# Hybrid encoder trunk: layer 0's output weights serve two chunks at once

## The chip, the cores and the metric

The kernel runs on one core of a Trainium2 chip. Its engines are TensorE (PE in the profile, with PEld for its weight loads), VectorE (DVE), ScalarE (ACT), GpSimd (POOL) and SyncE (SP), which here only issues DMA transfers. The metric is the device time of one execution in microseconds (us), lower is better; medians of several runs are compared.

## The reference

Two layers of a bidirectional encoder on a sequence of 2048 tokens with 1024 channels, in float32, then a final RMSNorm:

```python
def hybrid_layer(x, ...):
    h = rmsnorm(x, norm_g)
    proj = einsum("bsd,de->bse", h, w_in)            # 1024 -> 3584
    ...
    y_a = conformer_conv(a_u, a_v, ...) * silu(a_z)  # depthwise conv of width 31, LayerNorm
    y_b = short_gated_conv(b_b, b_c, b_x, ...) * silu(b_z)
    y_c = window_gqa(c_q, c_k, c_v, sink) * silu(c_z)        # window of +-128 tokens
    y_d = neighborhood_attn(d_q, d_k, d_v, rpb) * silu(d_z)  # 32 x 64 grid
    y = concatenate([y_a, y_b, y_c, y_d], axis=-1)   # 4 x 256 channels
    return x + einsum("bse,ed->bsd", y, w_out)       # 1024 -> 1024
```

## The kernel before

Channels lie on partitions, tokens along the free dimension. The 2048 tokens are four chunks of 512; chunks 0 and 1 are half 0, chunks 2 and 3 half 1. Within a half the text calls the first chunk A and the second B. The core's memory holds the operand of two chunks at a time, in two slots: tiles s0h and s0l for A, s1h and s1l for B, eight tiles of 128 channels each (kept in four pairs).

Float32 products are made of three matmuls in the faster format: each operand is split into a high part (a cast on ACT) and a low part (a subtraction on DVE), and high x high, high x low and low x high are added up in PSUM. Weights come in tiles of 128 output channels; each is loaded in two halves of 256 KB into a raw tile (`load_w`, tile wraw, line 882) and split into whi and wlo (`split_w`).

The main work is a list of jobs. A job takes one weight tile and one chunk (24 matmuls of 128x512) or both chunks of the half (a joint job, 48 matmuls, the same weights split once). The order of the list is fixed: input jobs of half 0 and of half 1 of layer 0, output jobs of half 0 (layer 0), input jobs of half 0 of layer 1, output jobs of half 1 (layer 0), input jobs of half 1 of layer 1, output jobs of layer 1. `run(j)` emits a job in groups of 8 matmuls. After each group stands a point (`point()`), at which the generators of all the other work emit their next step: evictions (`evs`), attention units (`units`), and work in the background (`bg`), such as fetching the next input. Attention of a chunk is made of 16 units, each a chain of scores (s), softmax, transposes (pt) and values (o). If a job's operand has not been emitted when the job's turn comes, `idle_until` emits points without matmuls until it has. A scheduler then orders each engine's instructions by its own estimate of when they can start, so they don't stand exactly as emitted.

An output job of layer 0 adds its PSUM tile to a tile of x (`ev_out`: tile xo, fetched by `xo_tile`), squares the sum on ACT, adds the square to an accumulator (tile acc, tag "sa"), and stores the new x. After a chunk's eighth output job, `rstd_steps` sums the squares over the channels on PE (cs) and forms the reciprocal root in 13 small DVE steps; `stage_steps` of layer 1 reloads x (tile xt), spreads the root on PE (rb), copies it (rs) and scales the eight tiles; `place_steps` splits them into the slot. These are hung on the last output job of each chunk:

```python
then(o00[0], lambda: stage_steps(1, 0), pl(1, 0, 0))
then(o00[1], lambda: stage_steps(1, 1), pl(1, 1, 1))
```

In the same way y of chunk A is placed after A's last input job and y of B after B's (`place_y_steps`: loads of s0l or s1l from the tensors Y, a cast, a subtraction), once attention, convolution and gates of that chunk are done (`y_ready`). The input jobs begin with 3 (layer 0) or 5 (layer 1) tiles for A alone and then for B alone, go on with joint jobs, and end with 3 tiles for A and then B.

Of the kernel before, what the change touches and what calls it, by code (L numbers as in the profile page):

```python
# [7 lines left out]
F32 = mybir.dt.float32  # L8
# [7 lines left out]
DEPTH = 2  # L16
SEQ = 2048
DM = 1024
P = 128
KT = DM // P  # L20
CH = 512
# [34 lines left out]
TB, TH, XTB, GA, GB = 5, 2, 4, 2, 4  # L56
QSB, PRB, PTB = 2, 4, 2
GRP = 8
RU, RU1, RD = 3, 5, 3
PF, UNITS, SPACING = 7, 4, 5  # L60
PF_LATE, UNITS_LATE, SPACING_LATE = 3, 6, 2
LEAD, LEAD_LATE = 6.0, 6.0
# [9 lines left out]
def trunk(ctx, tc, xT, w_in, w_out, par, sink, rpb, fg, trig, cmask, dmask, out):  # L72
# [3 lines left out]
    def mkpool(name, bufs=1, **kw):  # L76
        return ctx.enter_context(tc.tile_pool(name=name, bufs=bufs, **kw))
# [3 lines left out]
    wp = mkpool("wp")  # L81
    gp = mkpool("gp")
# [6 lines left out]
    def T(pool_, shape, dt, tag, bufs, name=None):  # L89
        uid[0] += 1  # L90
        return pool_.tile(shape, dt, tag=tag, bufs=bufs, name=f"{name or tag}_{uid[0]}")
# [13 lines left out]
    def xrows(src, k, c):  # L105
        return src[2 * k * P:(2 * k + 2) * P, cs(c)].rearrange("(k p) t -> p k t", p=P)
# [63 lines left out]
    evs, bg, units, taps = [], [], [], deque()  # L170
# [33 lines left out]
    def idle_until(cond):  # L204
        n = 0
        while not cond():
            point()
            clk["pe"] += 1.8
            n += 1
            assert n < 4000, "nothing more happens"  # L210

    def hold(n):
        for _ in range(n):
            yield
# [610 lines left out]
    stat = {}  # L825

    def xo_tile(l, c, dt):
        src = xT if l == 0 else LP[l - 1]["X"]
        if l == DEPTH - 1:
            if c % 2 == 0:  # L830
                if dt % 2 == 0:
                    held["xx"] = T(gp, [P, 2, CH], F32, "xt", XTB, "xf")
                    sp.dma_start(out=held["xx"], in_=xrows(src, dt // 2, c))
                return held["xx"][:, dt % 2]
            if dt >= 4:
                if dt % 2 == 0:
                    held["xg"] = T(gp, [P, GW], F32, "gA", GA, "xf")
                x = held["xg"][:, (dt % 2) * CH:(dt % 2) * CH + CH]
            else:
                x = T(gp, [P, CH + 3], F32, "gB", GB, "xf")[:, :CH]  # L840
        else:
            x = T(gp, [P, CH + 3], F32, "gB", GB, "xo")[:, :CH]
        sp.dma_start(out=x, in_=src[dt * P:(dt + 1) * P, cs(c)])
        return x

    xos = {}

    def ev_out(l, dt, c, pt):
        x = xos[(l, c, dt)]
        dve.tensor_tensor(out=x, in0=x, in1=pt, op=ALU.add)  # L850
        yield
        if dt == 0:
            acc = stat[(l, c)] = T(gp, [P, CH], F32, "sa", 1, "acc")
            act.activation(out=acc, in_=x, func=AF.Square)
        else:
            acc = stat[(l, c)]
            sq = T(gp, [P, CH], F32, "t", TB, "sq")
            act.activation(out=sq, in_=x, func=AF.Square)
            if dt < KT - 1:
                dve.tensor_tensor(out=acc, in0=acc, in1=sq, op=ALU.add)  # L860
        yield
        if l < DEPTH - 1:
            sp.dma_start(out=LP[l]["X"][dt * P:(dt + 1) * P, cs(c)], in_=x)
        if dt == KT - 1:
            yield from rstd_steps(l + 1, c, (acc, sq), ("rc", l + 1, c))
            if l == DEPTH - 1:
                yield
                rb = spread(RC[l + 1][:, 4 * c:4 * c + 4], CH)
                yield
                rs = rb  # L870
                for k in range(KT):
                    xk = xos[(l, c, k)]
                    dve.scalar_tensor_tensor(out=xk, in0=xk, scalar=fg_t[:, k:k + 1], in1=rs, op0=ALU.mult, op1=ALU.mult)
                    sp.dma_start(out=out[k * P:(k + 1) * P, cs(c)], in_=xk)
                    if k % 2:
                        yield


    def load_w(jb, hf):
        raw = T(wp, [P, 4, P], F32, "wraw", 4)  # L880
        jb.setdefault("raw", []).append(raw)
        sp.dma_start(out=raw, in_=jb["src"][:, 4 * hf:4 * hf + 4, :])

# [5 lines left out]
    jobs = []  # L889

    def job(src, keys, ev, pre=None, post=None):
        jobs.append({"src": src, "keys": keys, "ev": ev, "pre": pre, "post": post})
# [98 lines left out]
        return first, len(jobs) - 1  # L991

    def out_jobs(l, half):
        ends = []
        for c in ((0, 1), (2, 3))[half]:
            for dt in range(KT):
                def pre(dt=dt, c=c):
                    if l == DEPTH - 1 and c % 2:
                        idle_until(lambda: not taps)

                    def get():
                        yield from hold(2)
                        for d in ((0, 1, 2) if dt == 0 else (dt + 2,)):
                            if d < KT:
                                xos[(l, c, d)] = xo_tile(l, c, d)
                    bg.append(get())
                job(w_out[l, dt], [("y", l, c)], lambda c_, pt, dt=dt: ev_out(l, dt, c_, pt), pre, None)
            ends.append(len(jobs) - 1)
        return ends

    def y_ready(l, c):
        need = [(k, l, c, p, j) for k in "dc" for p in range(2) for j in range(4)]
# [197 lines left out]
```

## Time and profile before

| | us |
|---|---|
| Median of 3 runs | 2041.24 (2040.83 to 2048.28) |
| The profiled execution | 2040.77 |
| its span, first to last instruction | 2039.0 |
| PE busy in the span | 1959.9 |
| DVE busy | 1489.6 |
| ACT busy | 1043.3 |
| POOL busy | 150.5 |

PE is busy for 96% of the span and its mean granted clock is 0.986 of full speed. Matmuls overlap their successors, so a busy share counts a wait only from where the last matmul ends. 1.8 us of the execution lie outside the span.

### The profile page before, as it was taken

Reading aid. Unit: us, or ns where it says so; the run is one execution under the profiler, and the core shown is the slowest. Engines: PE = TensorE matmul, PEld = TensorE weight load, DVE = VectorE, ACT = ScalarE, POOL = GpSimd, SP = SyncE. Lnnn points to the kernel's source line nnn. Section 1 sums busy time; section 2 is a strip of 40 time slices with the busy share of each in tenths; the row PEclk is TensorE's granted clock in tenths of the full one; section 3 lists DMA queues with packets and bytes.
Section 4 is the critical chain, followed back from the end, with each engine's and each line's share of the span. In section 5 each row is a group of like instructions: output and inputs, shape, how many; then the busy total and the mean of one; then the engine's idle time right before and its main releaser. Section 6 shows DMA issues by size and latency. Waiting matters only on the chain.

```text
span 2039.0 us, 29509 instructions
## 1 busy us (share of the span) xinstructions
PE 1959.9 (96%) x9600; PEld 1642.2 (81%) x9600; DVE 1489.6 (73%) x3209; ACT 1043.3 (51%) x2219; POOL 150.5 (7%) x138
## 2 busy tenths in 40 slices
PE   6999999999999999999999999999999889989997
PEld 5778888778788888878888888888888778878886
DVE  7444699947985777776465999777986457877775
ACT  5335434423365456556564445644237455777632
POOL 0241000043010100000010000001001000100000
PEclk9999999999999999999999999999999999999998
DMA  6995532588356369877663446876446874678473
GB/s 208 294 332 184 148 111 84 171 265 263 129 176 195 123 193 298 268 229 232 208 201 121 141 142 203 266 237 222 136 147 210 236 203 130 195 226 238 150 266 119
DMA packets 235003, 402.76 MB, mean 198 GB/s; under 512 B 26977, under 2 KB 92129, under 8 KB 234593
## 3 DMA queue, kind: packets, MB, share of 16 engines
q1 hardware_dynamic: 234848, 400.87, 63.1%
q8 instruction: 77, 1.26, 0.3%
q14 instruction: 78, 0.63, 0.1%
HBM read 299.78 MB, written 105.61 MB: 199 GB/s over the span
## 4 chain that ended last, share of the span: by engine, by line
PE 75%; DMA 13%; DVE 6%; issue 2%; ACT 2%; SPq 1%; POOL 1%; DVEq 0%; ACTq 0%; POOLq 0%
PE mm L135 61%; PE o L135 4%; PE s L135 4%; PE pt L734 3%; DMA prob<-bias 2%; DMA wraw<-in_w_out_dram 2%; DMA s1l<-Y 2%; DVE wlo L128 1%; DVE accA L128 1%; PE cs L135 1%; POOL bmo L817 1%; PE rb L135 1%; DMA vt<-VD 1%; DMA Y<-accA 1%; DMA s0l<-Y 1%
## 5 line engine op out<-in xcount | busy, mean ns | idle before, releaser
L135 PE MATMUL mm<-s1h,whi 128*128 128x512 f32 x1152 | 458.3, 398 | 16.5 <-ACT whi L218 8.3
L135 PE MATMUL mm<-s1h,wlo 128*128 128x512 f32 x1152 | 456.8, 397 | 2.0 <-DVE wlo L128 1.9
L135 PE MATMUL mm<-s0h,whi 128*128 128x512 f32 x1152 | 453.9, 394 | 4.9 <-ACT whi L218 3.0
L135 PE MATMUL mm<-s1l,whi 128*128 128x512 f32 x1152 | 456.0, 396 | 0.0
L135 PE MATMUL mm<-s0l,whi 128*128 128x512 f32 x1152 | 454.3, 394 | 1.8 <-DVE s0l L128 1.8
L135 PE MATMUL mm<-s0h,wlo 128*128 128x512 f32 x1152 | 454.1, 395 | 0.4 <-DVE wlo L128 0.4
L218 ACT CAST whi<-wraw 128x512 fp32r<-128x512 f32 x408 | 251.8, 618 | 393.0 <-PE mm L135 294.6
L128 DVE TENSOR_TENSOR wlo<-wraw,whi 128x512 fp32r<-128x512 f32 x408 | 293.5, 721 | 161.3 <-ACT whi L218 149.1
L128 DVE SCALAR_TENSOR_TENSOR accA<-gA,par,accA 128x1024 f32<-128x1024 f32 (+1 forms) x240 | 309.0, 1305 | 0.7
L135 PEld LDWEIGHTS mm<-s1h,whi 128*128 128x128 f32 x1152 | 219.6, 191 | 62.2 <-ACT whi L218 9.5
L135 PEld LDWEIGHTS mm<-s1h,wlo 128*128 128x128 f32 x1152 | 219.6, 191 | 47.9 <-DVE wlo L128 3.8
L135 PEld LDWEIGHTS mm<-s1l,whi 128*128 128x128 f32 x1152 | 220.1, 191 | 44.5 <-issue 0.5
L135 PEld LDWEIGHTS mm<-s0h,whi 128*128 128x128 f32 x1152 | 217.4, 189 | 47.7 <-ACT whi L218 4.1
L135 PEld LDWEIGHTS mm<-s0l,whi 128*128 128x128 f32 x1152 | 217.4, 189 | 45.6 <-DVE s0l L128 2.5
L135 PEld LDWEIGHTS mm<-s0h,wlo 128*128 128x128 f32 x1152 | 217.5, 189 | 44.4 <-DVE wlo L128 2.1
L707 ACT ACTIVATE prob<-prob,mn 128x384 f32<-128x384 f32 (+4 forms) x256 | 155.5, 608 | 113.2 <-DVE mn L128 111.2
L724 ACT ACTIVATE prob<-prob,sm 128x384 f32<-128x384 f32 (+4 forms) x256 | 142.2, 603 | 39.7 <-DVE sm L128 33.9
L128 DVE TENSOR_TENSOR pth<-pt,pth 128x512 fp32r<-128x512 f32 (+3 forms) x248 | 138.0, 572 | 29.0 <-ACT pth L218 28.0
L218 ACT CAST pth<-pt 128x512 fp32r<-128x512 f32 (+3 forms) x248 | 115.1, 496 | 80.3 <-PE pt L734 46.5
L135 PE MATMUL s<-ks,qs 128*128 128x384 f32 (+4 forms) x512 | 128.3, 352 | 17.6 <-DVE mn L128 10.9
L135 PE MATMUL o<-pth,vt 128*128 128x256 f32 (+2 forms) x784 | 129.8, 292 | 2.2 <-DVE oy L128 0.5
L135 PEld LDWEIGHTS o<-pth,vt 128*128 128x128 f32 (+2 forms) x784 | 114.9, 193 | 13.3 <-ACT prob L707 1.6
(122 smaller groups left out, 2006.0 us busy)
## 6 DMA issues: line engine op xcount, KB each, us to landing
wraw<-in_w_in_dram SPq DMA_DIRECT2D x280, 256.0 KB
wraw<-in_w_out_dram SPq DMA_DIRECT2D x128, 256.0 KB
qs<-QD SPq DMA_DIRECT2D x128, 128.0 KB
qs<-QC SPq DMA_DIRECT2D x128, 128.0 KB
G<-g SPq DMA_DIRECT2D x48, 256.0 KB
vt<-VD SPq DMA_DIRECT2D x144, 72.0 KB
xt<-in_xT_dram SPq DMA_DIRECT2D x20, 512.0 KB
KD<-t SPq DMA_DIRECT2D x32, 256.0 KB
```

The lines of the kernel that those rows point to most:

```text
L128: return fn(*a, **kw)
L135: pe.matmul(out=out, lhsT=lhsT, rhs=rhs, start=start, stop=stop)
L218: act.copy(out=hi, in_=src)
L707: act.activation(out=t[:, hh, :n], in_=t[:, hh, :n], func=AF.Exp, bias=mn[:, hh:hh + 1], scale=-1.0, accum_out=sm[:, hh:hh + 1])
L724: act.activation(out=t[:, hh, :n], in_=t[:, hh, :n], func=AF.Copy, scale=sm[:, hh:hh + 1])
L734: pe.transpose(out=tp[:kw, b_, hh, :], in_=t[:, hh, kb * kw:(kb + 1) * kw], identity=ident)
L817: pool.tensor_tensor(out=t[:, hh, :sz].rearrange("p (g r c) -> p g r c", r=rr, c=C), in0=mkv, in1=Ms[2 * p + hh][:, r0:r0 + R, c0:c0 + C]. ...
```

## The change

The output jobs of a half of layer 0 were eight for A and then eight for B, each splitting its own weights. Now the first two tiles (RO = 2) are done for A and then for B, the next four as joint jobs, and the last two for A and then for B: 12 jobs in place of 16. Layer 1 keeps its order. Since both chunks' sums of squares are open at once, there are two accumulators; the memory for the second comes from the raw weight tiles, now three. The tile of x is fetched when its own job begins, not from two jobs ahead on.

```diff
-RU, RU1, RD = 3, 5, 3
+RU, RU1, RD, RO = 3, 5, 3, 2
...
-            acc = stat[(l, c)] = T(gp, [P, CH], F32, "sa", 1, "acc")
+            acc = stat[(l, c)] = T(gp, [P, CH], F32, "sa", 2, "acc")
...
-        raw = T(wp, [P, 4, P], F32, "wraw", 4)
+        raw = T(wp, [P, 4, P], F32, "wraw", 3)
...
     def out_jobs(l, half):
-        ends = []
-        for c in ((0, 1), (2, 3))[half]:
-            for dt in range(KT):
-                def pre(dt=dt, c=c):
-                    if l == DEPTH - 1 and c % 2:
-                        idle_until(lambda: not taps)
-
-                    def get():
-                        yield from hold(2)
-                        for d in ((0, 1, 2) if dt == 0 else (dt + 2,)):
-                            if d < KT:
-                                xos[(l, c, d)] = xo_tile(l, c, d)
-                    bg.append(get())
-                job(w_out[l, dt], [("y", l, c)], lambda c_, pt, dt=dt: ev_out(l, dt, c_, pt), pre, None)
-            ends.append(len(jobs) - 1)
-        return ends
+        A, B = ((0, 1), (2, 3))[half]
+        ends = {}
+
+        def emit(dt, cc):
+            def pre():
+                if l == DEPTH - 1 and dt >= 2:
+                    idle_until(lambda: not taps)
+                for c in cc:
+                    if (l, c, dt) not in xos:
+                        xos[(l, c, dt)] = xo_tile(l, c, dt)
+            job(w_out[l, dt], [("y", l, c) for c in cc], lambda c_, pt: ev_out(l, dt, c_, pt), pre, None)
+            for c in cc:
+                ends[c] = len(jobs) - 1
+
+        if l == DEPTH - 1:
+            for c in (A, B):
+                for dt in range(KT):
+                    emit(dt, (c,))
+            return ends[A], ends[B]
+        for c in (A, B):
+            for dt in range(RO):
+                emit(dt, (c,))
+        for dt in range(RO, KT - RO):
+            emit(dt, (A, B))
+        for c in (A, B):
+            for dt in range(KT - RO, KT):
+                emit(dt, (c,))
+        return ends[A], ends[B]
```

How this moves instructions is seen in the built programs, at three places. The first is on PE, in the output jobs of half 0. Before, the third job (mm_1456) goes on with chunk 0:

```order
L135 MATMUL o_1437_7270<-pth_1426_7222,vt_1247_6454 128x256 x2
L734 MATMUL pt_1446_7316<-ident_77,prob_1403_7115 120x128 x4
L734 MATMUL pt_1447_7321<-ident_77,prob_1403_7115 120x128 x2
L135 MATMUL mm_1456_7340<-s0h_1370_6997,whi_1442_7287 128x512
L135 MATMUL mm_1456_7340<-s0l_1374_7001,whi_1442_7287 128x512
```

Now the third and fourth jobs (mm_1493 and mm_1510) are chunk 1's. These rows stand where they begin on the second half of their channels, tiles s1h_1466 and s1l_1470, the third pair of chunk 1's y; mm_1528, of which a row stands ahead, is the fifth job's part for chunk 0:

```order
L135 MATMUL mm_1528_7636<-s0h_1371_6998,wlo_1512_7577 128x512
L135 MATMUL o_1482_7436<-pth_1478_7411,vt_1458_7353 128x256 x2
L734 MATMUL pt_1487_7468<-ident_77,prob_1459_7358 128x128 x4
L135 MATMUL o_1482_7436<-pth_1479_7414,vt_1458_7353 128x256 x2
L135 MATMUL mm_1493_7486<-s1h_1466_7382,whi_1451_7330 128x512
L135 MATMUL mm_1510_7562<-s1h_1466_7382,whi_1506_7554 128x512
L135 MATMUL mm_1493_7486<-s1l_1470_7386,whi_1451_7330 128x512
```

Chunk 1's y is read from the third job on, where before it was read from the ninth; the first halves of the third to fifth jobs and attention stand ahead of the second halves. From the first output matmul to the first row with s1h_1466 there are 84 matmuls of jobs and 70 of attention (8 s of 360 columns, 8 s of 512, 26 o, 28 pt).

The second place is on PE, from the output jobs of half 1 to the input jobs of layer 1. Before, the last output job (mm_2864) is followed by the first input job (mm_2872) directly:

```order
L135 MATMUL mm_2864_13744<-s1h_2639_12716,whi_2861_13738 128x512
L135 MATMUL mm_2864_13744<-s1l_2643_12720,whi_2861_13738 128x512
L135 MATMUL mm_2864_13744<-s1h_2639_12716,wlo_2862_13739 128x512
L135 MATMUL mm_2872_13790<-s0h_2819_13532,whi_2865_13756 128x512
L135 MATMUL mm_2872_13790<-s0l_2823_13536,whi_2865_13756 128x512
```

Now two jobs of chunk 3 stand between chunk 2's last output job and the first input job for chunk 2 (mm_2834), with chunk 2's cs between the two jobs, and its rb and chunk 3's cs behind them. These rows are the end of that cs and what follows:

```order
L135 MATMUL cs_2817_13668<-ones_78,acc_2698_13013 128x1
L135 MATMUL cs_2817_13668<-ones_78,sq_2815_13663 128x1
L135 MATMUL mm_2834_13745<-s0h_2824_13708,whi_2807_13625 128x512
L135 MATMUL mm_2849_13800<-s0h_2824_13708,whi_2835_13756 128x512
L135 MATMUL mm_2834_13745<-s0l_2828_13712,whi_2807_13625 128x512
```

Eight jobs stood between the two before; the first two input jobs (mm_2834 and mm_2849) now take the tiles in turn. From half 0 into layer 1 it is the same, with 33 matmuls of attention between (8 s, 12 pt, 13 o) beside two jobs, two cs and rb.

The third place is on SP, near the start. Before:

```order
L882 DMA wraw_45_297<-in_w_in_dram 128x512
L882 DMA wraw_50_317<-in_w_in_dram 128x512
L273 DMA xt_83_490<-in_xT_dram 128x2x512
L273 DMA xt_84_492<-in_xT_dram 128x2x512
L273 DMA xt_85_494<-in_xT_dram 128x2x512
L273 DMA xt_86_496<-in_xT_dram 128x2x512
L882 DMA wraw_58_362<-in_w_in_dram 128x512
```

And now:

```order
L882 DMA wraw_45_297<-in_w_in_dram 128x512
L273 DMA xt_83_490<-in_xT_dram 128x2x512
L273 DMA xt_84_492<-in_xT_dram 128x2x512
L273 DMA xt_85_494<-in_xT_dram 128x2x512
L273 DMA xt_86_496<-in_xT_dram 128x2x512
L882 DMA wraw_50_317<-in_w_in_dram 128x512
L882 DMA wraw_58_362<-in_w_in_dram 128x512
```

With one raw tile less, the load of wraw_50 stands behind four loads of x.

## Rows read from the trace of the kernel before

**Rows 1.** The page, part 1: busy time, share of the span and instructions of each engine.

```profile
PE 1959.9 (96%) x9600; PEld 1642.2 (81%) x9600; DVE 1489.6 (73%) x3209; ACT 1043.3 (51%) x2219; POOL 150.5 (7%) x138
```

**Rows 2.** Busy time by stretch: stretch, length, engines' us, granted clock, DMA share, GB/s.

```profile
765.00:888.00 123.00, 117.24 (x582) 97.41 (x581) 87.87 (x206) 73.97 (x154) 1.29 (x1) 0.99 0.90 280
1262.00:1380.00 118.00, 116.28 (x589) 97.62 (x587) 91.17 (x229) 66.10 (x136) 2.89 (x2) 1.00 0.80 247
880.00:890.00 10.00, 7.30 (x30) 5.80 (x31) 7.49 (x22) 7.12 (x17) 0.00 (x0) 0.83 0.80 277
```

**Rows 3.** PE's waits from 765 to 888 us: us in total, times, longest.

```profile
PE mm L135 <- ACT whi L218: 2.9, 2, 2.1
PE mm L135 <- DVE wlo L128: 1.9, 1, 1.9
```

**Rows 4.** The page, part 5: groups of instructions; after the bar busy us, mean ns.

```profile
L218 ACT CAST whi<-wraw 128x512 fp32r<-128x512 f32 x408 | 251.8, 618 | 393.0 <-PE mm L135 294.6
L128 DVE TENSOR_TENSOR wlo<-wraw,whi 128x512 fp32r<-128x512 f32 x408 | 293.5, 721 | 161.3 <-ACT whi L218 149.1
```

**Rows 5.** Timeline of PE, output jobs of half 0: start us, us, instruction.

```profile
765.51 0.47 PE L135 MATMUL mm<-s0h,whi 128*128 128x512 f32 x1
765.82 0.39 PE L135 MATMUL mm<-s0l,whi 128*128 128x512 f32 x1
766.05 0.39 PE L135 MATMUL mm<-s0h,wlo 128*128 128x512 f32 x1
...
779.29 0.64 PE L135 MATMUL s<-ks,qs 128*128 128x512 f32 x2
...
781.52 0.48 PE L135 MATMUL mm<-s0h,whi 128*128 128x512 f32 x1
```

**Rows 6.** Timelines of ACT, SP and DVE: chunk 1's y is cast, stored, split.

```profile
772.09 1.14 ACT L218 CAST s1h<-s1l 128x512 fp32r<-128x512 f32 x2 [0.23 <-DMA s1l<-Y]
...
788.37 0.42 SPq L782 DMA_DIRECT2D Y<-ag  x1
...
798.85 0.69 DVE L128 TENSOR_TENSOR s1l<-s1l,s1h 128x512 fp32r<-128x512 f32 x1 [4.83 <-ACT s1h L218]
```

**Rows 7.** Timelines of DVE, then SP: chunk 2 from its last eviction on.

```profile
1325.40 0.69 DVE L128 TENSOR_TENSOR xo<-xo,mm 128x512 f32<-128x512 f32 x1 [1.60 <-PE mm L135]
...
1333.27 0.16 DVE L128 TENSOR_SCALAR rn<-cs 128x4 f32<-128x4 f32 x1 [0.39 <-PE cs L135]
...
1335.64 0.17 DVE L128 TENSOR_SCALAR rc<-rc 128x4 f32<-128x4 f32 x1
...
1342.38 5.39 DVE L128 SCALAR_TENSOR_TENSOR xt<-xt,par,rs 128x512 f32<-128x512 f32 x8 [1.47 <-ACT rs L302]
...
1348.29 0.68 DVE L128 TENSOR_TENSOR s0l<-xt,s0h 128x512 fp32r<-128x512 f32 x1
...
1331.40 0.38 SPq L863 DMA_DIRECT2D X<-xo  x1
...
1335.84 0.38 SPq L273 DMA_DIRECT2D xt<-X  x1
```

**Rows 8.** Timeline of PE, chunk 0: sums over channels, and the root spread.

```profile
835.38 0.28 PE L135 MATMUL cs<-ones,acc 128*128 128x1 f32 x2
...
836.86 0.36 PE L135 MATMUL cs<-ones,sq 128*128 128x1 f32 x2
...
848.62 1.05 PE L135 MATMUL rb<-ident,rc 128*128 128x128 f32 x8
```

**Rows 9.** The page, part 5: two groups of attention.

```profile
L724 ACT ACTIVATE prob<-prob,sm 128x384 f32<-128x384 f32 (+4 forms) x256 | 142.2, 603 | 39.7 <-DVE sm L128 33.9
L128 DVE TENSOR_TENSOR pth<-pt,pth 128x512 fp32r<-128x512 f32 (+3 forms) x248 | 138.0, 572 | 29.0 <-ACT pth L218 28.0
```

**Rows 10.** Waits of SP's queue and of PE over the whole span.

```profile
SPq L882 <- DVE wlo L128: 384.3, 177, 10.9
PE mm L135 <- ACT whi L218: 11.3, 6, 3.1
```

## Prediction, on record before the changed kernel ran

> **What bounds the kernel now.** I read the page first: TensorE (PE) is busy for 1959.9 of 2039.0 us [rows 1], so time is to be had only where PE stands still, and time is lost wherever a change makes it stand still. Then I read the two stretches that the change rewrites: the output projection of half 0 of layer 0 (765 to 888 us, "out phase 0") and that of half 1 (1262 to 1380 us, "out phase 1"). PE is busy for 117.2 of 123 us in the one and for 116.3 of 118 us in the other, with the DMA engines at 0.90 and 0.80 [rows 2]. So 5.8 and 1.7 us are idle there. In phase 0 the list of PE's waits puts 2.9 us on the high halves of the weights (whi) and 1.9 us on the low halves (wlo) [rows 3]: late weights. Last I read the timelines at the edges of these phases, because the change moves when chunk B's y is first wanted, and when chunk A's x is done.
>
> **Prices.** A 128x512 matmul starts 0.23 us after the one before it (765.82 to 766.05), so a single job (24 of them) is 5.5 us; one attention unit's four s, six o and six pt matmuls take 779.29 to 781.52, 2.2 us, or 0.14 us each [rows 5]. The sums over columns (cs) take 835.38 to 837.22, 1.85 us, and the spread of the result (rb) 1.05 us [rows 8].
>
> **What is removed.** Eight jobs fewer are split, four in each half: 16 halves of weights, each a 256 KB load, a cast of 618 ns on ScalarE (ACT) and a subtraction of 721 ns on VectorE (DVE) [rows 4]: 9.9 us of ACT, 11.5 us of DVE, 4 MB. All of it lies beside PE and is worth only the waits it causes. The matmuls stay the same in number. I take it that the weight waits of phase 0 (2.9 + 1.9 us) go, with the drop of the clock behind them: from 880 to 890 us the granted clock averages 0.83 [rows 2], so 1.7 us are lost beside the wait. And the 1.7 us of phase 1 go. Together -8.2 us; bounds 0 and -11 (all idle time of both phases, 7.5, the clock, and 1.7 more just behind phase 0).
>
> By the Trainium skill, Perfetto Trace Analysis, section Identifying the Most-Contended Engine, the busy share of matmuls says little about what is left, and that of weight loads should be used. Weight loads are busy for 97.4 of 123 us in phase 0, which would leave 25.6 us to gain and give about 2015 us. The start-to-start times above contradict it here: a load is hidden under each 0.23 us matmul, and nothing is gained by shortening loads. The sum goes by the rows.
>
> **What is moved, place A: the third job of an out phase.** Before, chunk B's y was wanted after eight jobs; now after two. In phase 0 the first job starts at 765.5 us [rows 5]. By the changed order, 84 main matmuls (the two jobs, and the first halves of the third, fourth and fifth, which the scheduler has put ahead) and 70 of attention stand before the first that reads the third pair of B's tiles: 84 x 0.23 + 70 x 0.14 = 29.1 us, so PE is there at 794.6 us. The first two pairs are cast from 772.09 us on at the latest; the third waits for the store of group C's rows (788.37) and is split at 798.85 [rows 6]. PE waits 4.2 us. Lower bound 0, if attention's last unit of chunk 1 ends earlier with fewer matmuls around it; upper bound 10, if the three units now packed into these 29 us wait for DVE and ACT in turn. In phase 1 the changed order puts B's first matmuls between those of the second job, so that B's y hardly comes too late there: 0.5 us (0 to 3).
>
> **Place C: from phase 1 into layer 1.** Before, eight jobs of B (55 us) covered the making of A's next input; now two do. The chain in the trace: A's last eviction at 1325.40, squares, cs, thirteen small DVE steps from 1333.27 to 1335.81 (2.5 us), rb, a copy (rs), eight scalings (5.4 us from 1342.38), first split at 1348.29 to 1348.97 [rows 7]: 23.6 us in all, with waits for PE in it. In the new order, from A's last matmul: B's first job 5.5, cs 1.85, B's second job 5.5 (the 2.5 us of small steps lie under it), rb 1.05, copy 0.7, scalings 5.4, split 0.7: 20.7 us. PE has 5.5 + 1.85 + 5.5 + 1.05 + 1.85 (B's sums) + 0.5 = 16.2 us of work. It waits 4.5 us; bounds 3 and 10 (23.6 less two jobs and the sums). The last X store and the reload behind it took 4.4 us (1331.40 to 1335.84) plus the landing, and fit under B's two jobs. Behind the first split PE has six matmuls per tile (1.4 us; the order takes two jobs in turn) against 0.68 us for a split, so nothing more is lost.
>
> **Place B: from phase 0 into layer 1.** The same chain, with attention in the queues: on PE 0.7 us more in B's first job, 1.4 us in the second and 0.7 us behind it; on ACT two row scalings (603 ns) stand ahead of the copy; on DVE a softmax step and two subtractions (572 ns) stand between the scalings and the first split [rows 9]: 20.7 + 0.7 + 1.4 + 0.7 + 1.2 + 0.6 + 1.1 = 26.4 us. PE's share in it is 48 main matmuls, two cs, rb and 33 of attention: 11.0 + 3.7 + 1.05 + 4.6 + 0.5 = 20.8 us. It waits 5.6 us; bounds 0 and 12.
>
> **The clock.** The waits at A, B and C are each about as long as the two waits of phase 0 on weights together [rows 3], whose drop of the clock cost 1.7 us: 3 x 1.7 = 5.1 us (0 to 6.8).
>
> **Three raw weight tiles.** Every raw load may go out only when the half three (not four) before it is split, half a single job (2.7 us) later, in all 408 halves, and SP has whatever follows queued behind that wait: it waited for wlo 177 times, 384.3 us in all, with four tiles already [rows 10]. The work that hides it is the job in between. Where PE waits on weights already, a later load adds its 2.7 us: six times on whi, 11.3 us in all [rows 10]. Six times 2.7 is 16 us, the upper bound; lower bound 0. I take 2.5, about one of the six, since SP's waits show that even now loads go out as a tile comes free, and PE was late only these six times.
>
> **At nothing:** the second accumulator of squares (both chunks' are alive at once); the tile of x, now fetched by its own job and not two ahead (a store and reload of 256 KB took 4.4 us, under a job's 5.5; if later, DVE waits in the eviction and the weights' subtractions behind it wait too); PSUM, of which a joint job takes two of three buffers, as it did before in the input phases.
>
> **Sum.** 4.2 + 0.5 + 4.5 + 5.6 + 5.1 - 8.2 + 2.5 = +14.2 us. The profiled execution took 2040.8 us, 0.5 us below the median of the three runs (2041.2), so **2055 us**; this case's own range is 2044 to 2066.
>
> **The rivals.**
> - *The covers are thin* (0.12): the three places cost their upper bounds, 10 + 3 + 10 + 12 and 6.8 for the clock, +42; nothing of phase 0's waits is won: about 2084. For it speaks that the old chain took 23.6 us with no one in a hurry; against it, the order, which shows PE's other work standing ahead.
> - *The third raw tile was needed* (0.13): the six waits on weights each grow by 2.7 us, 16 in place of 2.5: 2069. The Trainium skill, DMA: Bandwidth & Descriptors, section Rules for kernel authors, bears on it: issue a DMA early and wait for it late. Against it: PE waited for whi only six times in 408 halves.
> - *It cancels* (0.22): with attention ahead and DVE lighter, A costs 0, B 2, C 4.5, one drop of the clock 1.7, and -8.2 is won: 2041.
> - *Faster* (0.08): A, B and C stay below 1 us in all, because B's y and A's x are ready when wanted, and the waits of both phases go (-10.9): 2030. It needs PE's work ahead of place C to be 4.5 us longer than the rows give, so I hold it unlikely. Of the chance, 0.02 stands for the 2015 us that the Trainium skill's measure would give.
> - The forecast has the rest, 0.45.
>
> About 0.5% (10 us) is what a measurement can tell from no change. Slower by more: the two slow rivals and three quarters of the forecast's range, 0.59; within: 0.33; faster: 0.08. The range leaves out about one in ten at each end: 2035 to 2080.
>
> **What would show it.** In the changed profile: 392 halves of weights cast (408 less 16); PE's waits on s1h or s1l at the third out job of half 0, and on s0h or s0l at the first two input jobs of layer 1 in both halves, 4 to 6 us each, with the clock low behind each; no whi or wlo wait at the end of phase 0. It is wrong if those waits are missing, or if PE waits on whi elsewhere by more than 16 us in all.

## The result, and the profile after

The changed kernel takes 2072.01 us (median of four, 2068.66 to 2075.44) against 2041.03 for the kernel before (four runs, 2038.89 to 2048.28): ratio 1.0145, 95% interval 1.0119 to 1.017. That is 31 us slower, where +14 was forecast. The page's busy times (columns as in [rows 1]) of the execution that was profiled, the slowest of the four, with a span of 2073.6 us:

```profile
PE 1972.1 (95%) x9600; PEld 1653.1 (80%) x9600; DVE 1476.7 (71%) x3193; ACT 1035.9 (50%) x2203; POOL 149.8 (7%) x138
```

PE runs the same 9600 matmuls as in [rows 1]. Its idle time in the span rose from 2039.0 - 1959.9 = 79.1 to 2073.6 - 1972.1 = 101.5 us (+22.4), and it is busy 12.2 us longer on the same work: that is the clock, whose mean fell from 0.986 to 0.978. DVE and ACT have less to do, as forecast (12.9 and 7.4 us), and the kernel is slower all the same. Busy times by stretch (out phase 0, layer 1 half 0, out phase 1, the rest), first of the kernel before, cut at the phases' ends, then of the changed one:

```profile
765.50:887.40 121.90, 116.14 (x575) 96.43 (x574) 86.94 (x202) 72.87 (x152) 1.29 (x1) 0.99 0.90 279
887.40:1262.70 375.30, 373.82 (x1894) 317.17 (x1892) 282.63 (x627) 209.66 (x479) 12.65 (x9) 1.00 0.58 179
1262.70:1379.50 116.80, 115.08 (x583) 96.88 (x583) 89.97 (x228) 64.97 (x134) 2.51 (x2) 1.00 0.80 250
1379.50:2039.00 659.50, 625.59 (x3109) 523.63 (x3107) 479.99 (x1098) 352.19 (x764) 26.01 (x20) 0.98 0.62 190
```

```profile
767.30:903.60 136.30, 127.77 (x651) 108.29 (x650) 87.18 (x224) 78.26 (x171) 1.30 (x1) 0.96 0.81 247
903.60:1293.80 390.20, 381.08 (x1879) 321.03 (x1878) 289.04 (x647) 214.20 (x489) 13.11 (x9) 0.98 0.57 174
1293.80:1411.00 117.20, 112.39 (x537) 93.54 (x537) 72.36 (x164) 48.96 (x90) 6.75 (x5) 0.97 0.67 217
1411.00:2073.60 662.60, 623.68 (x3092) 524.11 (x3092) 481.02 (x1104) 351.13 (x763) 19.29 (x16) 0.97 0.62 188
```

Out phase 0 grew by 14.4 us, but layer 1 half 0, in which no code was changed, by 14.9. Out phase 1 grew by 0.4 and the rest by 3.1; 1.8 us were lost before 767. Each kernel was traced once, and this first stretch took 760.7 to 770.2 us in the traces cut in this way, so that a few us in one stretch say little without the waits behind them. Over the three phases PE's idle time went from 9.0 to 22.5 us and its busy time from 605.0 to 621.2, with 15 matmuls more on record (3067 for 3052; attention runs earlier): 13.5 us of waits, and some 14 of clock (16.2, less 15 x 0.14 for these). What PE waited for in the first two stretches, in the third, and from 1411 to 1425 us:

```profile
PE mm L135 <- ACT s1h L218: 5.1, 1, 5.1
PE mm L135 <- DVE wlo L128: 2.5, 1, 2.5
PE cs L135 <- ACT sq L858: 0.6, 1, 0.6
...
PE o L135 <- DVE pth L128: 3.1, 2, 2.9
PE mm L135 <- ACT t L372: 2.2, 1, 2.2
PE s L135 <- DVE wlo L128: 1.8, 1, 1.8
...
PE mm L135 <- ACT whi L218: 4.4, 3, 3.9
...
PE mm L135 <- DVE s0l L128: 3.9, 1, 3.9
```

The first row is place A (796 us), the first of the second stretch place B (904 us, 2.9 of it), the last place C: the waits that were forecast. At place B what PE met first was not s0h or s0l but attention's pth (the split transposes), which DVE splits at 906.61 us, behind the scalings of chunk A's x. Three were not: wlo at 880 us, the waits on t and behind wlo between 959 and 970 us, and whi at 1310 us.

The new code also changes a thing in layer 1, whose order it keeps. There the wait for the last convolution steps (`taps`) stood ahead of every output job of B; now it stands ahead of every output job from the third tile on, of A and of B. The traces show no cost of it: layer 1's output jobs take 250.4 us in both kernels (1788.6 to 2039.0 and 1823.2 to 2073.6 us).

**The weights at 880 us.** In [rows 3] PE waits for whi and wlo, and the prediction took both for late weights. The two long ones stand in one place, and they have two causes. PE, then ACT, before:

```profile
880.84 0.50 PE L135 MATMUL mm<-s1h,whi 128*128 128x512 f32 x1 [2.07 <-ACT whi L218]
883.43 0.71 PE L135 MATMUL mm<-s1h,wlo 128*128 128x512 f32 x1 [1.86 <-DVE wlo L128]
880.17 0.62 ACT L218 CAST whi<-wraw 128x512 fp32r<-128x512 f32 x1 [4.11 <-DMA wraw<-in_w_out_dram]
```

The whi was late because its load was: the cast on ACT waited 4.11 us for it. The load went out on SP at 874.27 us, behind a fetch of xo at which SP had stood for 5.8 us, until a store of X was done (from 866 to 880 us):

```profile
SPq L843 <- DMA X<-xo: 5.8, 1, 5.8
```

In the changed kernel that wait on whi is gone. The wait on wlo is another matter, and DVE's timeline tells why. Before:

```profile
875.33 0.14 DVE L128 TENSOR_TENSOR es<-mn,sink 128x2 f32<-128x2 f32 x1
882.08 0.28 DVE L128 TENSOR_TENSOR oy<-o,ou 64x128 f32<-64x128 f32 x1 [6.61 <-issue]
882.10 0.06 DVE L128 MEMSET cx<- 128x2 f32 x1
882.37 0.28 DVE L128 TENSOR_TENSOR oy<-o,ou 64x128 f32<-64x128 f32 x1
882.69 0.69 DVE L128 TENSOR_TENSOR wlo<-wraw,whi 128x512 fp32r<-128x512 f32 x1
```

After:

```profile
871.96 0.28 DVE L128 SCALAR_TENSOR_TENSOR ag<-oy,ag 128x128 f32<-128x128 f32 x1
881.95 0.06 DVE L128 MEMSET cx<- 128x2 f32 x1 [9.70 <-DMA X<-xo]
882.02 0.69 DVE L128 TENSOR_TENSOR wlo<-wraw,whi 128x512 fp32r<-128x512 f32 x1
```

A memset of two columns (60 ns) for cx, the padded operand of a convolution some 300 us later, has been put into DVE's queue here. In the built program it stands ahead of oy and wlo in the kernel before too, though oy's record begins 20 ns earlier. Its buffer belongs to the ring (gB) that the tiles xo use, and comes free only when a store of X is done. All of DVE waits, with it the split of the next weights into wlo, and PE behind them. The Trainium skill, PSUM — Partial Sum Buffer, section Engine vs sequencer instructions, says that VectorE's queue is strictly first in, first out; the 9.7 us for a 60 ns instruction agree.

**The stop at 956 to 970 us.** PE's timeline between the second and the third input job of chunk B in layer 1 (the 87th of the list, as the expectations count):

```profile
955.61 0.39 PE L135 MATMUL mm<-s1h,wlo 128*128 128x512 f32 x1
955.83 0.52 PE L135 MATMUL s<-ks,qs 128*128 128x384 f32 x2
...
958.14 0.38 PE L414 MATMUL tv<-ident,vt 128*128 128x128 f32 x2
...
961.14 1.04 PE L135 MATMUL s<-ks,qs 128*128 128x288 f32 x4 [1.84 <-DVE wlo L128]
963.04 0.69 PE L734 MATMUL pt<-ident,prob 128*128 128x128 f32 x2 [0.87 <-DVE hv L128]
...
964.12 1.11 PE L414 MATMUL tv<-ident,vt 128*128 128x128 f32 x4
...
966.10 1.48 PE L734 MATMUL pt<-ident,prob 128*96 128x128 f32 x6
969.77 0.79 PE L135 MATMUL mm<-s1h,whi 128*128 128x512 f32 x1 [2.19 <-ACT t L372]
```

For 14 us no job runs, only attention and the transposes of v (tv). These belong to chunk A's third input job: ACT copied its result (vt) at 929.6 us, and its tv runs at 958.1. In the kernel before the two were 912.7 and 918.5. Before, then after (windows 905 to 985 and 920 to 1000 us):

```profile
L414 PE MATMUL tv<-ident,vt x16: 270/272/273, 918.5 to 965.6; 128*128 128x128 f32 x16
...
L414 PE MATMUL tv<-ident,vt x16: 270/272/473, 958.1 to 993.5; 128*128 128x128 f32 x16
```

The tiles tv take turns with attention's own transposes in a ring of two PSUM buffers ("pt"), and here two late attention units stand ahead. Behind tv the chain goes on: its result (hv) is split and stored, its buffer lets ACT empty the PSUM tile of A's fifth job (t, which waited 1.08 us for that store), and that PSUM tile is what B's third job needs. The clock fell with it:

```profile
962.10:975.80 13.70, 10.49 (x33) 8.31 (x33) 7.40 (x20) 8.80 (x21) 0.00 (x0) 0.50 0.91 272
```

0.50 of full speed, 1.2 GHz, for 13.7 us, of which PE was busy 10.5.

**The wait at 1310 us** is made on ACT: the cast of whi (1313.24) stands behind casts of chunk 3's y, which wait 2.57 us for their load, and then waits 0.90 us for its own.

```profile
1311.21 1.14 ACT L218 CAST s1h<-s1l 128x512 fp32r<-128x512 f32 x2 [2.57 <-DMA s1l<-Y]
1313.24 0.62 ACT L218 CAST whi<-wraw 128x512 fp32r<-128x512 f32 x1 [0.90 <-DMA wraw<-in_w_out_dram]
```

### The profile page after: what moved, and what is told of

It is laid out like the page before. It is cut to its first block, busy times and chain, and to the rows that moved or that the text cites. A ratio compares the mean times of both kernels' runs of the same rounds, so it can differ in the third digit from the quotient of the medians.

```text
span 2073.6 us, 29400 instructions
## 1 busy us (share of the span) xinstructions
PE 1972.1 (95%) x9600; PEld 1653.1 (80%) x9600; DVE 1476.7 (71%) x3193; ACT 1035.9 (50%) x2203; POOL 149.8 (7%) x138
## 4 chain that ended last, share of the span: by engine, by line
PE 78%; DMA 12%; DVE 5%; issue 2%; ACT 1%; POOL 1%; SPq 1%; DVEq 0%; POOLq 0%; ACTq 0%
PE mm L135 64%; PE o L135 4%; PE s L135 4%; PE pt L734 3%; DMA prob<-bias 2%; DMA wraw<-in_w_in_dram 1%; DMA rep<-in_rpb_dram 1%; DMA VD<-hv 1%; DVE accA L128 1%; POOL bmo L817 1%; DMA bm<-rep 1%; DVE xt L128 1%; DVE wlo L128 1%; DMA s0l<-Y 1%; PE rb L135 1%
## 5 line engine op out<-in xcount | busy, mean ns | idle before, releaser
L218 ACT CAST whi<-wraw 128x512 fp32r<-128x512 f32 x392 | 242.0, 618 | 414.2 <-PE mm L135 296.9
L128 DVE TENSOR_TENSOR wlo<-wraw,whi 128x512 fp32r<-128x512 f32 x392 | 280.2, 716 | 187.3 <-ACT whi L218 174.5
L135 PE MATMUL o<-pth,vt 128*128 128x256 f32 (+2 forms) x784 | 131.7, 294 | 4.8 <-DVE pth L128 3.4
```

Source lines behind the costliest of these rows:

```text
L128: return fn(*a, **kw)
L135: pe.matmul(out=out, lhsT=lhsT, rhs=rhs, start=start, stop=stop)
L218: act.copy(out=hi, in_=src)
```

## The experiments

The theories, as the expectations number them. 1: the edges (places A, B, C) cost the time, and what follows them. 2: the third raw weight tile. 3: the planner (the code of `run`, `point` and `idle_until`, which lays the program out before it runs) starts attention units at the points at which it waits for staged operands, and the chip can't keep up. 4: the zero fill of cx. 5: the PSUM ring that v's transposes share with attention. Ratios are to the kernel before, run beside each.

### Two terms by themselves

**e1.**

```diff
-        raw = T(wp, [P, 4, P], F32, "wraw", 4)
+        raw = T(wp, [P, 4, P], F32, "wraw", 3)
```

> The kernel before with three raw weight tiles in place of four, and nothing else changed. If the edges of the out phases cost the time (theory 1), this is worth what the changed kernel had lost when it reached its first out phase, 1.5 us at 766 us, and about as much again behind it: 2041 to 2046 us. If the third raw tile was needed (theory 2), the six waits on weights grow by 2.7 us each and more appear: 2055 us or above.

2041.23 us, ratio 0.9992 (0.997 to 1.0014). With three tiles in place of four nothing is lost that can be measured; theory 2 falls, and with it the rival of 2069 us, as far as the old order can show it.

**e16** (the kernel before, too).

```diff
-                    def get():
-                        yield from hold(2)
-                        for d in ((0, 1, 2) if dt == 0 else (dt + 2,)):
-                            if d < KT:
-                                xos[(l, c, d)] = xo_tile(l, c, d)
-                    bg.append(get())
+                    xos[(l, c, dt)] = xo_tile(l, c, dt)
```

> The kernel before, but each out job fetches its own tile of x at its start and not two jobs ahead, as the changed kernel does. If that is hidden under the job's 5.5 us, as the prediction said: no change, 2039 to 2045. If it holds the evictions and VectorE's queue behind them: 16 jobs of the first layer by about a microsecond, 2050 or above.

2043.47 us, 1.001 (0.999 to 1.003): nothing in the old order, as the prediction had it.

### The edges moved

**e2 and e3**: `RE` tiles apart at the end in place of RO; e2 has RO, RE = 2, 4, and e3 has 4, 2.

```diff
-        for dt in range(RO, KT - RO):
+        for dt in range(RO, KT - RE):
             emit(dt, (A, B))
         for c in (A, B):
-            for dt in range(KT - RO, KT):
+            for dt in range(KT - RE, KT):
```

> The changed kernel with two joint jobs in each out phase in place of four: two tiles apart at the start as now, and four apart at the end, so that four jobs of chunk B follow chunk A's last. Theory 1 (edges): the waits at places B and C go (2.9 + 0.6 and 3.9 us, with half clocks of 6.8 and 6.8 us behind them, some 14 us together), and with A's and B's staging apart the backlog of attention at 956 to 970 us goes too (some 12 us); place A stays. 2040 to 2055 us, layer 1 half 0 taking 375 us again and not 390. Theory 2 (raw tile): 2065 to 2075, as the changed kernel.

> The changed kernel with two joint jobs in each out phase, four tiles apart at the start and two at the end. Theory 1 (edges): place A's wait (5.1 us and 1.7 us of clock) goes or halves, places B and C and the backlog of attention behind B stay: 2062 to 2070 us, layer 1 half 0 still taking about 390 us. Theory 2 (raw tile): 2065 to 2075. A theory that the backlog comes from place A (attention driven ahead while chunk B's y is awaited) would have layer 1 half 0 back at 375 us, and the time at 2045 to 2055.

e2: 2082.32 us, 1.0208 (1.0172 to 1.0245), slower, against theory 1. The trace shows chunk A's sums and its spread result now between B's jobs, and PE waiting there, 3.2 us for cs and 3.3 for rb; layer 1 half 0 still took 391 us, and v's first tv ran 31 us after its job. So the bunching of both chunks' staging is not what makes the stop. e3: 2069.07 us, 1.0137 (1.0106 to 1.0169), all but unchanged. Place A's wait is gone, out phase 0 is down to 127.5 us, layer 1 half 0 took 386 us.

**e7 and e12**: the new order in one half alone (`if l == DEPTH - 1 or half == 1:` takes the old path in e7, `half == 0` in e12).

> The changed kernel with the new order in out phase 0 alone; out phase 1 is as before, tile by tile, chunk A and then B. By the two traces out phase 0 and the input phase behind it lost 14.4 + 15.0 us and everything from out phase 1 on 5 us. If the losses stand where the traces put them (theory 1): 2064 to 2070 us, and the last third of the program as in the kernel before. If the two phases share a cause that either one sets off, or the later phases only drift with the first: 2050 or below, or 2072 unchanged.

> The changed kernel with the new order in out phase 1 alone; out phase 0 tile by tile, chunk A and then B. With the new order in half 0 alone the time was 2074.5, as much as in both. If half 1's new order costs what its edges show (3.9 us at 1310, 3.9 at place C, and 3.4 us each for the clock, less 1.7 of waits before): 2048 to 2054. If the removed loads and casts pay for them: 2040 to 2046.

e7: 2074.52 us, 1.0144 (1.0126 to 1.0162), above its range: half 0 alone loses as much as both. Its out phase 1, in the old order again, takes 121.6 us. e12: 2057.71 us, 1.0086 (1.0057 to 1.0114), above both of its ranges. The halves don't add (0.0144 and 0.0086, and 0.0145 for both). Out phase 1 of e12:

```profile
1269.00:1396.40 127.40, 123.77 (x600) 103.70 (x599) 82.86 (x214) 61.38 (x127) 7.22 (x5) 0.95 0.71 218
```

127.4 us with 600 matmuls, against 117.2 with 537 in the changed kernel: with the old order in half 0, more of attention falls into out phase 1, beside the new order's waits (there and at place C 2.3 us for wlo, 3.6 for s0l).

### The two causes that were not forecast

**e5 and e6**: the zero columns of cx, bg and gA, five places alike; e5 is the kernel before with it, e6 the changed one.

```diff
+    def zero(o, pt):
+        dve.tensor_scalar(out=o, in0=pt[:, 0:o.shape[1]], scalar1=0.0, scalar2=None, op0=ALU.mult)
...
-            dve.memset(cx[:, 0:2], 0.0)
+            zero(cx[:, 0:2], pt)
```

> The kernel before, but the zero columns at the edges of cx, bg and gA (2, 1 and 30 or 15 columns, 60 to 80 ns each) are written as 0 times the matmul's result in place of a memset, so that VectorE can't reach them before that matmul. In the kernel before such a memset of cx stands in VectorE's order at 882 us, some 300 us ahead of its use, and VectorE stands still for 6.6 us ahead of it; PE waits 2.07 and 1.86 us for whi and wlo just then. If these waits came from the memset (theory 4), they go with the 1.7 us of clock behind them: 2041 less 5.6, about 2035 us. If they came from late loads of weights, as the prediction had it, they stay: 2041.

> The changed kernel with the same edit. There VectorE stands still for 9.7 us ahead of the memset (872 to 882 us), and PE then waits 2.5 us for wlo, 0.6 for the sums, 2.9 at place B. If the memset alone makes them, and VectorE's backlog makes that of attention at 956 to 970 us too (theory 4): 2.5 + 0.6 + 2.9 + 5 us of idle time and some 10 us of clock less, 2050 to 2056 us. If the memset only covers waits that come anyway, and the bunched staging makes the backlog (theory 1): 2.5 + 1.7 us less, 2065 to 2069.

e5's out phase 0, and the wait on whi at its end:

```profile
762.50:881.50 119.00, 115.41 (x580) 95.58 (x578) 83.41 (x196) 69.77 (x147) 1.29 (x1) 1.00 0.90 281
...
878.25 0.50 PE L135 MATMUL mm<-s1h,whi 128*128 128x512 f32 x1 [1.61 <-ACT whi L218]
```

Idle 3.6 us in place of 5.8, the clock at 1.00. The wait on wlo is gone, so it was the memset's, and DVE no longer stands still for 6.6 us; of the wait on whi 1.61 of 2.07 us stay, and the cast still waits 3.66 us for its load: this one was not. The expectation set one cause against the other; each has one of the two waits. The total is 2042.28 us, ratio 1.0 (0.9985 to 1.0016): in the profiled execution the 2.9 us won here are lost again in the next two phases (378.0 and 122.0 us, for 375.3 and 116.8). e6: 2064.03 us, 1.0095 (1.008 to 1.0111). Its out phase 0 is 131.7 us with 6.0 idle, but layer 1 half 0 keeps its loss (390.4), and tv still runs 29 us late. PE's wait on wlo in out phase 0 is gone here too. Theory 4 holds for that wait, not for the stop; of some 10 us that e6 wins by the ratios, the traces put 4.6 into out phase 0.

**e4** (no unit begun at a planner's wait) and **e8** (tv in another ring), each on the changed kernel.

```diff
-            point()
+            point(False)
...
-        if waiting and gap[0] >= pace["spacing"] and len(units) < pace["units"] and begun[0] < turn[0] + QSB:
+        if begin and waiting and gap[0] >= pace["spacing"] and len(units) < pace["units"] and begun[0] < turn[0] + QSB:
```

> The changed kernel, but where the planner waits for staged operands (10 points at the third out job of half 0, 11 at the first input job of layer 1) it starts no further attention unit. If the planner's push of attention makes the backlog at 956 to 970 us (theory 3), layer 1 half 0 is back at 375 to 380 us and the time at 2055 to 2062. If the bunched staging of both chunks makes it (theory 1), nothing or little is won: 2066 to 2078.

```diff
-        tp = T(ps, [P, CH], F32, "pt", 2, "tv")
+        tp = T(ps, [P, CH], F32, "s", 2, "tv")
```

> The changed kernel with the transposes of v (tv) in the PSUM ring of the scores (s, two buffers) in place of that of attention's transposes (pt, two buffers). In the changed kernel the first tv of layer 1 runs 28.5 us after the job that it belongs to has ended (before: 6 us), behind two attention units in the pt ring, and input job 87 waits for the buffers that it frees (969.6 us). If this queue makes the stop at 956 to 970 us (theory 5), it goes with the 13.7 us of half clock: 10 us less, about 2062. If attention itself is late and PE has nothing else to do there: unchanged, 2066 to 2078.

Layer 1 half 0 in e4, then in e8:

```profile
895.30:1277.30 382.00, 373.72 (x1855) 314.93 (x1854) 288.05 (x636) 211.40 (x477) 13.61 (x9) 0.99 0.58 174
```

```profile
902.10:1283.40 381.30, 375.79 (x1878) 317.89 (x1877) 290.61 (x650) 212.84 (x489) 13.09 (x9) 0.99 0.59 178
```

Both win 8 to 9 of the 14.9 us. In e4 the first vt is copied at 923.2 us and tv runs at 926.2; in e8 at 929.2 and 941.0. Out phase 0 had 40 score matmuls before, 52 in the changed kernel, and 46 in e4. So attention driven ahead makes the queue, and the ring is where PE meets it. Only half of the 12 score matmuls more (three units) come from the planner's waits, by e4's 46; where the other half comes from is not shown. e8 takes 2060.63 us, 1.0071 (1.005 to 1.0092), some 15 us less than the changed kernel. e4 takes 2066.99, 1.012 (1.0084 to 1.0155), inside the range that its expectation gave to theory 1, with an interval that overlaps the changed kernel's: what layer 1 half 0 wins, out phase 1 partly takes back (124.1 us for 117.2), where the units not begun earlier now run.

### What is left

**e9**: the changed kernel with e6's and e8's edits; **e10**: with e4's as well; **e11**: the kernel before with e5's and e8's.

> The changed kernel with both edits, the zero columns pinned behind their matmul and tv in the ring of the scores. Alone they won about 10 us (2064) and 15 us (2060.6). If they cure two different losses (VectorE held at the end of out phase 0; v's transposes queued behind late attention in layer 1): some 20 to 25 us less than the changed kernel, 2047 to 2053, which leaves about what the prediction gave the edges (A, B, C and their clock, 17 us at most). If both only move the same loss: about 2060.

> The same, and the planner starts no attention unit at the points where it waits for staged operands (21 of them in half 0, which in the changed kernel put three units more, 12 score matmuls, into out phase 0). If attention ahead of what the chip can finish is the cause of the queue (theory 3), the ring edit has already cured what it costs, and this wins little more: 2044 to 2053. If the two are separate, another 5 us: 2042 to 2048.

> The kernel before with the zero columns pinned and tv in the ring of the scores. There v's transposes wait too (6 to 20 us behind their jobs), but PE stands still for only 1.5 us in layer 1 half 0. If the ring costs only where attention is late (theories 3 and 5): 2039 to 2045, no change. If it costs everywhere: 2035 or below, and this is the fastest version.

e9: 2053.12 us, 1.0066 (1.0043 to 1.0089). It is 0.0079 off the changed kernel's ratio, where e6 took 0.0050 and e8 0.0074: with the ring changed, the zero fill's pin wins nothing more that can be measured. 13.5 us (0.0066 x 2041.4) stay. Its waits in out phase 0, in layer 1 half 0 and from there to 1420 us:

```profile
PE mm L135 <- ACT s1h L218: 4.6, 1, 4.6
...
PE o L135 <- DVE pth L128: 3.7, 1, 3.7
...
PE mm L135 <- DVE s0l L128: 3.9, 1, 3.9
```

Places A, B and C, 12.2 us; the other waits in these three views add up to 4.1 us. e10: 2058.98 us, 1.0096 (1.0065 to 1.0126), above both of its ranges: nothing more is won. e11: 2040.08 us, 1.001 (0.9993 to 1.0026): before the change the two edits win nothing that can be measured.

**e13 and e14**: e9 with the new order in half 0 or half 1 alone. **e15, e17 and e18**: e9 with RO, RE = 4, 2; 2, 4; 4, 4. The last has no joint job.

> The changed kernel with both edits, and the new order in out phase 0 alone. If the rest is the edges: A and B with their clock, 4.6 + 3.7 + 3 to 5 us, and nothing for C: 2046 to 2052. If it comes from out phase 1 and place C alone: 2040 to 2044.

> The same with the new order in out phase 1 alone. If the rest is the edges: C with its clock (3.9 + 3 to 5 us), A's likeness in phase 1 at most 2: 2045 to 2052. If half 0 has it all: 2040 to 2044.

> The changed kernel with both edits and four tiles apart at the start of each out phase, two joint jobs, two tiles apart at the end. If the edges are the rest: place A's wait (4.6 us) and the clock behind it (6.8 us at half rate, 3.4 us lost) go, B and C stay: 2044 to 2048. If the rest is spread over everything that is new: 2050 to 2055.

> The changed kernel with both edits (zero columns pinned, tv in the ring of the scores) and two tiles apart at the start, two joint jobs, four tiles apart at the end. If e2's loss was the zero fill and the ring, and four jobs of B cover A's next input: places B and C go (3.7 and 3.9 us and their clock), 2042 to 2048. If four jobs at the end cost something of their own: 2055 or above.

> The same with four tiles apart at the start and four at the end, so that no job serves both chunks and no weight is shared; only the order of tiles differs from the kernel before. If sharing weights wins nothing and the edges are all: 2039 to 2046, as the kernel before. If the removed loads and casts are worth something under the edges' losses: slower than e15 and e17, 2050 or above.

| | median us | ratio | 95% interval |
|---|---|---|---|
| e9: 2 apart at the start, 2 at the end | 2053.12 | 1.0066 | 1.0043 to 1.0089 |
| e13: half 0 alone | 2050.88 | 1.0043 | 1.0024 to 1.0062 |
| e14: half 1 alone | 2061.12 | 1.0097 | 1.0072 to 1.0121 |
| e15: 4 and 2 | 2048.69 | 1.0031 | 1.0014 to 1.0048 |
| e17: 2 and 4 | 2055.87 | 1.0071 | 1.0049 to 1.0093 |
| e18: 4 and 4, nothing shared | 2051.04 | 1.0048 | 1.0029 to 1.0066 |

e15 takes place A away and wins about what A and its clock cost (7 us by the ratios, whose intervals just overlap); its out phase 0 is 125.2 us with 2.5 idle. In its one trace, though, the slowest of its runs, layer 1 half 0 is 5.6 us longer than e9's (385.6). e17 wins nothing at places B and C: PE no longer waits there for pth and s0l, but with four jobs of B behind A's last, chunk A's cs stands between them, and PE waited 5.1 us for it, because ACT had A's last square queued behind a cast of weights that waited 7.4 us for its load. The cover was longer, and another wait took the place. e18 fits neither expectation: with nothing shared, the order still costs 0.48%, and it isn't slower than e17. Its trace loses 7.3 us in out phase 0 (129.2) and 10.3 in layer 1 half 0 (385.6), though PE's waits at places A and C are down to 0.7 us for s1h and 0.3 for s0l, and v's first tv runs 6 us after its copy, as before. So a win or a loss by sharing the weights shows in none of these runs; e18 differs from e17 in the start as well, and from e15 in the end, so that none of them takes the sharing by itself. e13 came in its first range. e14 missed: half 1 alone costs no less than both halves. Its profile shows the longer out phase 1 of e12 (125.8 us); behind it the rest takes 672.2 us for 659.5, of which 3.9 are place C's wait and 8.4 lie in layer 1's output jobs (258.8 us for 250.4, the clock at 0.95 for 0.98). Why, is open. No version is measurably faster than the kernel before.

## Why the prediction was wrong

It had the direction; the size was less than half of what came. 2072 us lie above the 2044 to 2066 that the forecast gave its own case, and inside the wide range of 2035 to 2080. The rival of 2069 us came closest in number, by a mechanism that e1 finds to cost nothing: a coincidence. The sum failed at three steps.

- **"I take it that the weight waits of phase 0 (2.9 + 1.9 us) go" (-8.2).** Failed for the greater part. The long wait on whi (2.07 of the 2.9) was a late load; both waits on whi are gone, but no run shows that the fewer loads did it. The wait on wlo (1.9) was not a matter of how many weights there are: a zero fill held DVE for 6.6 us (e5). It stands in the changed kernel too, holds DVE for 9.7 us, and PE waits 2.5 us at the same place; with it the drop of the clock stays (3.4 us at half speed, in both kernels). The 1.7 us of phase 1 became 4.4. The view that would have told it was at hand: DVE's own idle time ahead of that split, with nothing else in its timeline.
- **Place B, and what is queued behind it.** The wait itself was 2.9 us, and 0.6 for the sums, for a forecast of 5.6. The step took attention as 33 matmuls that stand ahead (4.6 us) and nothing behind. What it left out came 50 us later: three units more are begun in out phase 0, half of them at the planner's two waits; they are late on the chip, v's transposes queue behind them in a PSUM ring of two, and a job behind those. 14.9 us in layer 1 half 0, of which e4 and e8 each take back 8 to 9; with both of e9's edits the phase takes 380.0 us.
- **The clock (3 x 1.7, less 1.7).** Mis-sized. Over the three phases it cost some 14 us. The stops are more than three (the two unforeseen ones have theirs), and one stretch at 1.2 GHz lasted 13.7 us, in which PE ran small matmuls between waits.
- **Place A (4.2)**: 5.1 us, and 4.6 in e9. **Place C (4.5)**: 3.9 for s0l and 0.4 for the sums. Both near, and e15 shows A's by taking it away.
- **Phase 1's likeness of A (0.5, bounds 0 to 3)**: 3.9 us, by a way that the step did not look at: PE met it as late weights, whose cast stood behind those of B's y on ACT. In e9 it is not there (0.2 us for whi from 1279.8 to 1420).
- **Raw tiles (2.5)**: nothing, in the old order (e1). The Trainium skill, DMA: Bandwidth & Descriptors, section Rules for kernel authors, would have a load issued early; one half job later was early enough here.
- **"At nothing"**: right for the tile of x, in the old order (e16). In the new order neither it nor the raw tiles were tried by themselves.

Of the signs that were named: 392 casts came, and the waits at A and C; at B it was attention's pth that PE met first; "no whi or wlo wait" in phase 0 held for whi and failed for wlo; PE's waits on whi are 18.6 us in all, above the 16 of the sign as it is worded, and 7.3 more than before (11.3 [rows 10]).

```profile
L218 ACT CAST whi<-wraw 128x512 fp32r<-128x512 f32 x392 | 242.0, 618 | 414.2 <-PE mm L135 296.9
PE mm L135 <- ACT whi L218: 18.6, 7, 5.2
```

With both unforeseen causes taken out, e9 still loses 13.5 us, and its largest waits are the prediction's three edges. That this is near the forecast of 14.2 is luck in part, since the forecast took 8.2 off for the removed work and put 2.5 on for the raw tiles. And that the edges make the 13.5 us is argued, not shown: e18 has next to no wait at places A and C and loses 0.48% all the same, and e14, with one of the three edges, loses no less than both halves.

Open are the rest of layer 1 half 0 (e9's 380.0 us against 375.3, of which place B is 3.7), why the order without sharing costs 0.48% in e18, why half 1 alone costs no less than both halves (e14), and what sharing the weights is worth by itself.

## What to carry to other kernels

When a busy engine waits for an operand, look at what the engine that makes it did just before. Of two waits on weights 2 us apart here, one was a late load, and the other a tiny instruction at the head of that engine's queue, waiting for a buffer that has nothing to do with weights; against the second, having fewer weights wins nothing. With PE busy for 96%, taking work off other engines has little to win, and a change of order moves waits; price not only the wait at the seam, but what the planner emits while it waits, and which rings of buffers that work shares with the main path. Give several short stops in a row a price for the clock that grows with their number.

## What the runs showed of the hardware

One drop of the clock came without a wait that the profile counts. PE's timeline and the granted clock in out phase 1 of the changed kernel:

```profile
1351.36 3.87 PE L135 MATMUL lnv<-ones,lns 128*128 128x1 f32 x32
1355.10 0.77 PE L135 MATMUL mm<-s0h,wlo 128*128 128x512 f32 x1
1355.67 0.63 PE L135 MATMUL mm<-s0h,whi 128*128 128x512 f32 x1
1356.10 0.63 PE L135 MATMUL mm<-s0l,whi 128*128 128x512 f32 x1
```

```profile
1354.60:1358.00 3.40, 3.40 (x11) 2.82 (x11) 2.88 (x18) 0.03 (x1) 0.00 (x0) 0.50 0.34 111
```

Behind 32 matmuls of one column each, in which PE counts as busy, the clock, at full speed since 1317.0 us, stood at 0.50 (1.2 GHz) for 3.4 us, and the 512-column matmuls started 0.43 us apart (1355.67 to 1356.10) instead of 0.23. PE's timeline shows no idle time between 1334.6 and 1355.1 us.
